# Two-layer hybrid backbone: modulation blocks moved between engines and stages

## The chip, the cores and the metric

One core of one Trainium2 chip runs the whole program in one launch. The metric is device time in microseconds. The kernel before takes 2973.64 us, the median of three runs (2973.43 to 2979.33).

## The reference

Two layers work on 256 latent tokens of width 2048. The first layer mixes with a gated linear recurrence beside a short convolution, the second with a Hyena long convolution; each is followed by a squared-ReLU feed-forward block of width 8192. All of it is fp32. What matters here:

```
sh1, sc1, g1, sh2, sc2, g2 = split(silu(c) @ ada_w[l] + ada_b[l], 6)     # per layer l
h = rmsnorm(x, norm_g[l, 0]) * (1 + sc1) + sh1
x = x + g1 * mixer(h)
x = x + g2 * square(relu((rmsnorm(x, norm_g[l, 1]) * (1 + sc2) + sh2) @ mlp_w1[l])) @ mlp_w2[l]
```

`ada_w` is 2 x 2048 x 12288 fp32 and is multiplied by one single vector per layer, so it is mostly a matter of streaming 192 MB. The Hyena filters come from a small network of position codes (`hyena_filters`: three layers of width 64 with sines, independent of the data).

## The kernel before, in words

**Stages.** The input projection and recurrence of layer 0; its output projection `ab_out`; feed-forward block `mlp(0)` (the first of the two); `hyena`, the third stage; then its output projection at the end of `hyena`; and `mlp(1)`, the second feed-forward block.

**Matrix products.** Weights arrive as 1 MB pieces `raw` (three buffers). ScalarE rounds each half to `whi`, VectorE forms the rest `wlo` (L151, L152), and TensorE makes three products of them with the split activations. In a feed-forward block `gemm_as` (L287) takes four such pieces for 512 outputs, and calls a hook after every piece. `mlp_body` goes through the hidden width in four quarters (`c`), with four passes of the first product and four of the second in each.

**Modulation blocks.** `ada_w` is cut into 192 blocks of 1 MB. Block number idx is l * 96 + ch * 16 + kt. A block whose number is not in `ON_PE` is a dot product on VectorE: one instruction of 2048 elements per partition with an accumulated output (L182). A block in `ON_PE` goes to TensorE instead: `ada_mm` makes 16 products of 32 output rows (L212), ScalarE copies the result out into `adas` (two buffers), and a later small product with `selr` sums the four row groups (L194), followed by an addition on VectorE (L195). These last two steps wait in a list, and `ada_flush` issues them at the next pump.

**Pumps.** All blocks from 32 on stand in one queue. `pump(n)` takes n of them, but never past `ada_stop`; `pump_rate(r)` adds r to a credit and pumps its whole part. The rates stand in `RATES`: ("m1", l) and ("m2", l) for the hooks of the feed-forward block of layer l, "hy" for the projections of the third stage. `pump_until` takes what a step needs. Before the change blocks 72 to 159 go to VectorE in `ab_out` (8) and in the first feed-forward block (80), 160 to 183 to TensorE in the third stage, and 184 to 191 to VectorE in the second feed-forward block. The loads go through SyncE's DMA queue, into `araw` (two buffers) in the feed-forward blocks and into `raw` elsewhere.

**Border of a feed-forward block.** `norm_apply` first makes the reciprocal root of the mean square (one small product, then twelve short VectorE instructions), then 16 tiles of three instructions on VectorE and ScalarE, which the first `gemm_as` waits for.

**Filter network.** `filter_net` runs two layers of the filter network on GpSimd alone, in compensated fp32 arithmetic, from the first stage on (L1050 to L1110, then a sine, L1159 to L1184). `filter_tail` is called in `mlp_body(0)` at c == 2, g == 0, before the second product of the third quarter: it transposes the result `fxn` on TensorE (L1127), multiplies (L1131), runs another sine on GpSimd in two halves and splits the outcome on VectorE (L1141, L1142).

**Order.** Each engine's instruction order is fixed at build time by a planner that goes by estimated times, dependences and the order of writing; on the chip each engine runs its own list strictly in order. `hold` ties a dot product behind the VectorE instruction written just before it.

Of the kernel before, what the change touches and what calls it, by code (L numbers as in the profile page):

```python
# [12 lines left out]
F32 = mybir.dt.float32  # L13
# [8 lines left out]
P = 128  # L22
D = 2048
# [4 lines left out]
LEVELS = (1, 2, 4, 8, 16, 32, 64)  # L28
KBLOCKS = (1, 2, 5, 8)
G = 2  # L30
RATES = {"gc": 0.35, "ab": 0.62, "y": 0, "gate": 0, "leash": 4, "tl": 1, "lo": 0.3, "hy": 0.5, "ho": 0.0, "ahead": 2,
         ("m1", 0): 0.65, ("m2", 0): 0.65, ("m1", 1): 0.15, ("m2", 1): 0.15}
SB = 8
ON_PE = set(range(32)) | set(range(56, 72)) | set(range(160, 184))

SM = {}
_o = 0
# [26 lines left out]
class Kernel:  # L64
# [111 lines left out]
    def ada_block(self, l, ch, kt):  # L176
# [3 lines left out]
        r = self.ada_load(l, ch, kt)  # L180
        if idx not in ON_PE:
            self.hold(nc.vector.scalar_tensor_tensor(out=r, in0=r, scalar=0.5, in1=self.sil, op0=ALU.mult,  # L182
# [236 lines left out]
    def norm_apply(self, l, i, slot):  # L419
        nc = self.nc  # L420
        bc = self.norm_rstd([self.ssum])
        self.new_h()
        a = l * 96 + i * 48
        for kt in range(KT):
            t = self.tmp(T, "cv0", 2)
            sh = self.mod[:, a + kt:a + kt + 1]
            nc.vector.scalar_tensor_tensor(out=t, in0=self.x[:, kt, :], scalar=self.gv[:, slot, kt:kt + 1], in1=bc,
                                           op0=ALU.mult, op1=ALU.mult)
            nc.scalar.activation(out=self.hhi(kt), in_=t, func=AF.Identity, bias=sh)  # L429
            nc.vector.scalar_tensor_tensor(out=self.hlo(kt), in0=t, scalar=sh, in1=self.hhi(kt).bitcast(F32),  # L430
                                           op0=ALU.add, op1=ALU.subtract)
# [4 lines left out]
    def build(self):  # L436
        nc, cp, I, tc = self.nc, self.cp, self.I, self.tc
        self.setup()
        with ExitStack() as st:
            self.pm = st.enter_context(tc.tile_pool(name="pm", bufs=1))  # L440
            with ExitStack() as sa:
                self.pa = sa.enter_context(tc.tile_pool(name="pa", bufs=1))
                self.layer0()
            with ExitStack() as sb:
                pb = sb.enter_context(tc.tile_pool(name="pb", bufs=1))
                self.make_sil(pb)
                self.ada_raw = lambda: pb.tile([P, D], F32, tag="araw", name="araw", bufs=2)
                self.pump_to(72)
                self.ada_stop = 160
                self.ab_out()  # L450
                self.mlp(0)
                self.ada_raw = None
        with ExitStack() as st:
            self.ph = st.enter_context(tc.tile_pool(name="ph", bufs=1))
            self.ada_stop = 184
            self.hyena()
        with ExitStack() as st:
            pb = st.enter_context(tc.tile_pool(name="pc", bufs=1))
            self.make_sil(pb)
            self.ada_raw = lambda: pb.tile([P, D], F32, tag="araw", name="araw", bufs=2)  # L460
            self.ada_stop = 192
            self.mlp(1)

    def layer0(self):
# [414 lines left out]
        for i in range(NH):  # L879
            acc = self.gemm(w1[16 + 3 * i], self.hhi, self.hlo, T)  # L880
            u = self.tmp(T, "cv0", 2)
            nc.scalar.activation(out=u, in_=acc[:, :T], func=AF.Copy)
            self.pump_rate(RATES["gc"])
            acc = self.gemm(w1[17 + 3 * i], self.hhi, self.hlo, T)
            nc.vector.tensor_tensor(out=u, in0=acc[:, :T], in1=u, op=ALU.mult)
            c = self.tmp(T, "cv1", 2)
            self.conv(u, c, self.s_("cw", i), self.s_("cw", 8 + i), self.s_("cw", 16 + i))
            self.pump_rate(RATES["gc"])
            acc = self.gemm(w1[18 + 3 * i], self.hhi, self.hlo, T)
            nc.vector.tensor_tensor(out=c, in0=acc[:, :T], in1=c, op=ALU.mult)  # L890
            self.hilo(c, self.uhi(8 + i), self.ulo(8 + i))
            self.pump_rate(RATES["gc"])
        self.drain()
# [5 lines left out]
    def ab_out(self):  # L899
        I = self.I  # L900
        for nt in range(KT):
# [3 lines left out]
            if nt < 13:  # L905
                self.pump_rate(RATES["ab"])
        self.dump("x0a", self.x)
# [73 lines left out]
    def mlp_body(self, l):  # L981
# [6 lines left out]
        for c in range(4):  # L988
            self.new_u()
            for g in range(4):  # L990
                rate = RATES["m1", l] if c or g else 0
                acc = self.gemm_as(I["m1"][l, c * 4 + g], self.hhi, self.hlo, lambda: self.pump_rate(rate))
# [6 lines left out]
            for g in range(4):  # L999
                if c == 3 and g == 2:  # L1000
                    self.pump_to(self.ada_stop)
                if c == 2 and g == 0 and l == 0:
                    self.filter_tail()
                rate = RATES["m2", l] if c < 3 or g < 3 else 0
                acc = self.gemm_as(I["m2"][l, c, g], self.uhi, self.ulo, lambda: self.pump_rate(rate))
# [465 lines left out]
def layout(a):  # L1471
# [6 lines left out]
    d["ada"] = c(a["ada_w"].reshape(2, D, 96, P).transpose(0, 2, 3, 1).reshape(192, P, D))  # L1478
    for i in ON_PE:
        blk = a["ada_w"][i // 96].reshape(KT, P, 96, P)[:, :, i % 96]  # L1480
# [55 lines left out]
```

## Time and profile before

The profiled execution took 2974.1 us; its span, from the first to the last instruction, is 2972.0 us.

| engine | busy us | share of the span |
|---|---|---|
| TensorE products | 2790.1 | 94% |
| TensorE weight loads | 2457.8 | 83% |
| VectorE | 2176.5 | 73% |
| ScalarE | 1246.6 | 42% |
| GpSimd | 1565.0 | 53% |

DMA moves 646 MB at a mean of 218 GB/s. The mean granted TensorE clock is 0.973 of full speed. Shares over the span mix stages with different limits, so the stage table in the rows below says more; a wait is always put down to the instruction that released it, and engine names in the rows are PE (TensorE), DVE (VectorE), ACT (ScalarE), POOL (GpSimd).

### The profile page before, as it was taken

Reading aid. Unit: us, or ns where it says so; the run is one execution under the profiler, and the core shown is the slowest. Engines: PE = TensorE matmul, PEld = TensorE weight load, DVE = VectorE, ACT = ScalarE, POOL = GpSimd, SP = SyncE. Lnnn points to the kernel's source line nnn. Section 1 sums busy time; section 2 is a strip of 40 time slices with the busy share of each in tenths; the row PEclk is TensorE's granted clock in tenths of the full one; section 3 lists DMA queues with packets and bytes.
Section 4 is the critical chain, followed back from the end, with each engine's and each line's share of the span. In section 5 each row is a group of like instructions: output and inputs, shape, how many; then the busy total and the mean of one; then the engine's idle time right before and its main releaser. Section 6 shows DMA issues by size and latency. Waiting matters only on the chain. (4 is left out here: it accounts for less than half of the span.)

```text
span 2972.0 us, 46189 instructions
## 1 busy us (share of the span) xinstructions
PE 2790.1 (94%) x18508; PEld 2457.8 (83%) x18508; DVE 2176.5 (73%) x2648; ACT 1246.6 (42%) x1660; POOL 1565.0 (53%) x1716
## 2 busy tenths in 40 slices
PE   5887999999989999998999899999989999999997
PEld 4777999889977888886888899998988888888885
DVE  4766659998798878876778899999765555545455
ACT  3221224343435444343444445545445444344443
POOL 5999999999999999997000445455100000000000
PEclk8998999999999999999999999999999999999998
DMA  5776545446757888875887445444545555555542
GB/s 206 279 264 237 189 145 191 160 153 235 259 216 269 320 304 302 312 297 224 315 308 267 169 159 182 168 182 166 196 170 199 218 217 187 187 182 189 186 180 110
DMA packets 97863, 646.48 MB, mean 218 GB/s; under 512 B 11673, under 2 KB 15833, under 8 KB 22257
## 3 DMA queue, kind: packets, MB, share of 16 engines
q1 hardware_dynamic: 96464, 640.35, 57.7%
q0 software_dynamic: 1184, 3.18, 0.7%
q8 instruction: 145, 2.38, 0.3%
q14 instruction: 70, 0.57, 0.1%
HBM read 641.39 MB, written 2.10 MB: 217 GB/s over the span
## 5 line engine op out<-in xcount | busy, mean ns | idle before, releaser
L152 DVE TENSOR_TENSOR wlo<-raw,whi 128x1024 fp32r<-128x1024 f32 (+1 forms) x778 | 1020.3, 1315 | 531.7 <-ACT whi L151 529.9
L151 ACT ACTIVATE whi<-raw 128x1024 fp32r<-128x1024 f32 (+1 forms) x806 | 843.5, 1049 | 1102.3 <-PE acc L287 713.3
L1030 POOL TENSOR_TENSOR xT<-xT,rstd 128x256 f32<-128x256 f32 x6 | 5.2, 900 | 853.3 <-DVE rstd L318 853.3
L287 PE MATMUL acc<-whi,hh 128*128 128x512 f32 x1024 | 403.2, 398 | 15.0 <-ACT hh L429 15.0
L266 PE MATMUL acc<-hh,whi 128*128 128x258 f32 (+1 forms) x1408 | 408.7, 290 | 0.0
L287 PE MATMUL acc<-whi,hl 128*128 128x512 f32 x1024 | 402.7, 398 | 3.1 <-DVE hl L430 3.1
L287 PE MATMUL acc<-whi,uh 128*128 128x512 f32 x1024 | 405.3, 396 | 0.0
L287 PE MATMUL acc<-whi,ul 128*128 128x512 f32 x1024 | 404.8, 395 | 0.0
L266 PE MATMUL acc<-hh,wlo 128*128 128x258 f32 (+1 forms) x1408 | 401.2, 285 | 3.4 <-DVE wlo L152 3.2
L266 PE MATMUL acc<-hl,whi 128*128 128x258 f32 (+1 forms) x1408 | 399.4, 284 | 0.0
L287 PE MATMUL acc<-wlo,uh 128*128 128x512 f32 x1024 | 282.0, 396 | 8.9 <-DVE wlo L152 8.9
L287 PE MATMUL acc<-wlo,hh 128*128 128x512 f32 x1024 | 280.1, 395 | 0.0
L266 PEld LDWEIGHTS acc<-hh,whi 128*128 128x128 f32 x1408 | 267.9, 190 | 7.4 <-issue 6.7
L266 PEld LDWEIGHTS acc<-hh,wlo 128*128 128x128 f32 x1408 | 267.5, 190 | 6.1 <-DVE wlo L152 4.2
L266 PEld LDWEIGHTS acc<-hl,whi 128*128 128x128 f32 x1408 | 269.0, 191 | 1.1 <-issue 0.9
L287 PEld LDWEIGHTS acc<-whi,hh 128*128 128x128 f32 x1024 | 193.4, 189 | 60.2 <-ACT hh L429 15.8
L182 DVE SCALAR_TENSOR_TENSOR araw<-araw,sil 128x2048 f32<-128x2048 f32 x96 | 237.9, 2479 | 0.2 <-DMA araw<-in_ada 0.2
L287 PEld LDWEIGHTS acc<-wlo,uh 128*128 128x128 f32 x1024 | 192.8, 189 | 54.1 <-DVE wlo L152 9.4
L287 PEld LDWEIGHTS acc<-whi,hl 128*128 128x128 f32 x1024 | 193.3, 189 | 47.4 <-DVE hl L430 4.7
L287 PEld LDWEIGHTS acc<-wlo,hh 128*128 128x128 f32 x1024 | 193.4, 189 | 45.4
L287 PEld LDWEIGHTS acc<-whi,uh 128*128 128x128 f32 x1024 | 193.0, 188 | 45.4 <-issue 0.3
L287 PEld LDWEIGHTS acc<-whi,ul 128*128 128x128 f32 x1024 | 193.0, 188 | 44.8
(358 smaller groups left out, 5803.3 us busy)
## 6 DMA issues: line engine op xcount, KB each, us to landing
raw<-in_m SPq DMA_DIRECT2D x256, 1024.0 KB, 4.8
araw<-in_ada SPq DMA_DIRECT2D x96, 1024.0 KB, 5.3
raw<-in_ada SPq DMA_DIRECT2D x93, 1024.0 KB, 4.9
raw<-in_w SPq DMA_DIRECT2D x71, 1024.0 KB, 4.9
raw<-in_hy SPq DMA_DIRECT2D x48, 1024.0 KB, 4.8
raw<-in_ho SPq DMA_DIRECT2D x16, 1024.0 KB, 4.8
raw<-in_w SPq DMA_DIRECT2D x12, 640.0 KB, 6.6
fr<-in_fw SPq DMA_DIRECT2D x16, 256.0 KB, 5.1
```

The costliest lines, as they stand in the source:

```text
L151: nc.scalar.activation(out=hi[:, :w], in_=src, func=AF.Copy)
L152: e.tensor_tensor(out=lo[:, :w], in0=src, in1=hi[:, :w].bitcast(F32), op=ALU.subtract)
L182: self.hold(nc.vector.scalar_tensor_tensor(out=r, in0=r, scalar=0.5, in1=self.sil, op0=ALU.mult, op1=ALU.mult, accum_out=self.mod[:, idx:i ...
L266: m = nc.tensor.matmul(acc[:, :n], lhsT=w[:, s], rhs=x(kt, n), start=hn == 0 and j == 0 and pn == 0, stop=hn == 1 and j == 7 and pn == 2).ins
L287: nc.tensor.matmul(acc[th], lhsT=x(kt)[:, th * P:(th + 1) * P], rhs=w[:, j * 512:(j + 1) * 512], start=kt == 0 and w is hi and x is xhi, s ...
L1030: e.tensor_tensor(out=self.x[:, nt, :], in0=self.x[:, nt, :], in1=rstd, op=ALU.mult)
```

## The change

Blocks 160 to 183 leave the third stage: the first feed-forward block now takes the queue up to 184. Of its 104 blocks the first six (80 to 85) go to TensorE, issued in one pump inside `norm_apply`, right after the small product and the reciprocal root; the other 98 are dot products, at a rate of 0.84 instead of 0.65 per hook. The third stage pumps nothing. The last eight blocks (184 to 191) go to TensorE in the second feed-forward block: six in `norm_apply`, two by rate. That block no longer builds the vector `sil`, which only dot products use, and has four `araw` buffers instead of two. The host lays a block of `ada_w` out by whether it is in `ON_PE`.

```diff
-RATES = {"gc": 0.35, "ab": 0.62, "y": 0, "gate": 0, "leash": 4, "tl": 1, "lo": 0.3, "hy": 0.5, "ho": 0.0, "ahead": 2,
-         ("m1", 0): 0.65, ("m2", 0): 0.65, ("m1", 1): 0.15, ("m2", 1): 0.15}
+RATES = {"gc": 0.35, "ab": 0.62, "y": 0, "gate": 0, "leash": 4, "tl": 1, "lo": 0.3, "hy": 0.0, "ho": 0.0, "ahead": 2,
+         ("m1", 0): 0.84, ("m2", 0): 0.84, ("m1", 1): 0.15, ("m2", 1): 0.15}
 SB = 8
-ON_PE = set(range(32)) | set(range(56, 72)) | set(range(160, 184))
+ON_PE = set(range(32)) | set(range(56, 72)) | set(range(80, 86)) | set(range(184, 192))
...
     def norm_apply(self, l, i, slot):
         nc = self.nc
         bc = self.norm_rstd([self.ssum])
+        self.pump(6)
         self.new_h()
...
                 self.pump_to(72)
-                self.ada_stop = 160
+                self.ada_stop = 184
                 self.ab_out()
                 self.mlp(0)
...
             pb = st.enter_context(tc.tile_pool(name="pc", bufs=1))
-            self.make_sil(pb)
-            self.ada_raw = lambda: pb.tile([P, D], F32, tag="araw", name="araw", bufs=2)
+            self.ada_raw = lambda: pb.tile([P, D], F32, tag="araw", name="araw", bufs=4)
             self.ada_stop = 192
             self.mlp(1)
```

## Rows read from the trace of the kernel before

**Rows 1.** Windows by stage: busy PE, PEld, DVE, ACT, POOL, then PEclk, DMA, GB/s.
```profile
905.00:1344.00 439.00, 439.00 (x1940) 356.29 (x1938) 361.47 (x293) 201.93 (x232) 431.83 (x374) 1.00 0.81 306
...
1405.00:1640.00 235.00, 233.15 (x1069) 191.26 (x1069) 185.99 (x219) 107.55 (x135) 5.19 (x3) 0.99 0.76 289
1640.00:2130.00 490.00, 455.66 (x4194) 440.42 (x4192) 443.54 (x641) 243.50 (x395) 224.55 (x153) 0.98 0.46 171
...
2207.00:2224.00 17.00, 7.96 (x27) 6.03 (x26) 14.14 (x32) 5.95 (x11) 0.00 (x0) 0.70 0.17 62
2224.00:2948.00 724.00, 724.00 (x3205) 588.28 (x3204) 375.44 (x364) 331.58 (x388) 0.00 (x0) 1.00 0.52 189
```

**Rows 2.** Dot products (line 182), 866:1344 and 1344:1405 us: min/median/max ns, starts.
```profile
L182 DVE SCALAR_TENSOR_TENSOR araw<-araw,sil x51: 2372/2548/2831, 905.2 to 1341.9; 128x2048 f32<-128x2048 f32 x51
L182 DVE SCALAR_TENSOR_TENSOR araw<-araw,sil x5: 2372/2551/2553, 1341.9 to 1383.4; 128x2048 f32<-128x2048 f32 x5
```

**Rows 3.** Waits of TensorE, 870 to 1600 us: total, times, longest.
```profile
PE acc L287 <- DVE wlo L152: 8.9, 1, 8.9
PE acc L287 <- ACT hh L429: 8.7, 1, 8.7
PE aux L1127 <- POOL fxn L1184: 4.7, 1, 4.7
```

**Rows 4.** Timeline of GpSimd: start, duration, line, tiles.
```profile
932.36 2.51 POOL L1055 TENSOR_TENSOR fwl<-fw,fwh 128x128 f32<-128x128 f32 x1
...
938.64 2.51 POOL L1101 TENSOR_TENSOR ft<-fp,ft 128x128 f32<-128x128 f32 x1
...
1313.90 0.46 POOL L1101 TENSOR_TENSOR ft<-fp,ft 128x128 f32<-128x128 f32 x1
...
1325.79 2.14 POOL L1164 TENSOR_TENSOR sfp<-sfp,sfe 128x128 f32<-128x128 f32 x1
...
1392.54 0.46 POOL L1164 TENSOR_TENSOR sfp<-sfp,sfe 128x128 f32<-128x128 f32 x1
```

**Rows 5.** Timeline of VectorE at the same times.
```profile
932.00 2.55 DVE L182 SCALAR_TENSOR_TENSOR araw<-araw,sil 128x2048 f32<-128x2048 f32 x1
...
938.28 2.55 DVE L182 SCALAR_TENSOR_TENSOR araw<-araw,sil 128x2048 f32<-128x2048 f32 x1
```

**Rows 6.** Timelines at the filter tail: GpSimd, VectorE and TensorE.
```profile
1348.74 0.42 PE L1127 MATMUL aux<-ident,fxn 128*64 128x128 f32 x1 [4.70 <-POOL fxn L1184]
...
1358.45 0.30 POOL L1159 TENSOR_SCALAR sfp<-cv 128x128 f32<-128x128 f32 x1 [9.77 <-DVE cv L1133]
...
1403.71 0.29 DVE L1141 CAST h3h<-cv 128x256 fp32r<-128x256 f32 x1 [14.36 <-POOL cv L1184]
...
1406.85 2.07 PE L287 MATMUL acc<-wlo,uh 128*128 128x512 f32 x4 [8.92 <-DVE wlo L152]
```

**Rows 7.** Third stage: windows of L212, of tile adas; L195; in the chain, shares.
```profile
1640.00:2130.00 490.00, 28.05 (x768) 20.67 (x768) 0.98 0.46 171
1640.00:2130.00 490.00, 6.68 (x48) 7.39 (x48) 6.50 (x24) 0.98 0.46 171
L195 DVE TENSOR_TENSOR mod<-aux,sm x40: 141/146/159, 451.5 to 2115.2; 128x1 f32<-128x1 f32 x40
2104.78 1.01 PE aux L212 x32
by line: DVE p L931 13.4%; DVE wlo L152 12.7%; DVE yl L158 8.3%; issue 7.2%; DVE y L1332 6.6%; POOL H L1270 4.5%; DVE tf L1247 4.1%; DVE p L933 4.0%; DVE cv L1298 3.6%; DVE y L1330 3.5%; DVE Z L1270 3.3%; ACT whi L151 2.7%; ACT p L928 2.6%;
by line: PE acc L266 33.7%; PE aux L1344 6.4%; DVE wlo L152 6.4%; DVE yl L158 6.2%; PE aux L1209 5.9%; DVE p L931 5.0%; DVE y L1332 4.2%; issue 3.4%; DVE cv L1298 3.4%; DVE y L1330 3.3%; DVE Z L1270 2.5%; PE aux L212 2.0%; POOL tf L1259 2.0
```

**Rows 8.** Timeline of TensorE at the border of the second feed-forward block.
```profile
2217.40 1.22 PE L287 MATMUL acc<-whi,hh 128*128 128x512 f32 x2 [6.37 <-ACT hh L429]
...
2222.50 0.63 PE L287 MATMUL acc<-whi,hh 128*128 128x512 f32 x2
...
2225.28 0.63 PE L287 MATMUL acc<-whi,hh 128*128 128x512 f32 x2
```

## The prediction, made before the change was timed

> **What bounds the kernel now.** I read the stage table first, then the waits of TensorE, then the timelines around the longest waits. The table [rows 1] is to be read by stage, since every stage has another limit. In the first feed-forward block up to 1344 us TensorE is busy all the time (439.0 of 439.0 us), VectorE 361.5 us, and GpSimd 431.8 us: GpSimd, too, has nothing left. The reader is to see that two engines are full here, and that VectorE's 18% of idle time is shared by both of them. From 1405 us to the end of that block GpSimd is idle and TensorE full. In the third stage (1640 to 2130 us) neither TensorE (455.7 of 490) nor VectorE (443.5) is full. The second block (2224 to 2948) is TensorE's alone.
>
> The waits of TensorE in the first block [rows 3] are three: 8.7 us at its border for the first normalized rows, 4.7 us for `fxn`, and 8.9 us behind VectorE. The last two are one matter. GpSimd works since the first stage on the small network that makes the Hyena filters (`filter_net`); `filter_tail`, which stands at the start of the third quarter's second product, needs its result. TensorE comes to that place at 1344.0 and GpSimd ends at 1348.7 [rows 6]. So the end of this stretch is set by GpSimd already, by a margin of 4.7 us; TensorE's full row before it hides that.
>
> **What a dot product costs GpSimd.** This is the term on which my forecast rests. A modulation dot product on VectorE lasts 2.55 us while GpSimd works [rows 2, 5]. The GpSimd instruction that meets it lasts 2.51 us, where the same line takes 0.46 us with VectorE idle [rows 4, 5]: 2.05 us lost; for the shorter dot product at 1325 it is 2.14 against 0.46, 1.68 us lost [rows 4]. I take 1.9 us per dot product.
>
> The Trainium skill has a rule on this (SBUF — State Buffer, "Who interferes with whom"): a VectorE instruction with two SBUF inputs and a GpSimd one that reads SBUF exclude each other, and the second fully blocks. Taken by the letter, a dot product costs GpSimd all of its 2.55 us, the term below would be 36.7 instead of 27.4 us, and the whole 3001 us. The rows say less, because one GpSimd instruction's own work is let through with each.
>
> **The change part by part.**
>
> *More dot products before the tail.* `filter_tail` comes after 20 matrix passes of 4 pumps each, the first four without a rate: 76 pumps. At 0.65 they bring 49 dot products (the trace has 51 between 905 and 1344 us [rows 2], two having slipped ahead); at 0.84 they bring 64. That is 14.4 more (76 x 0.19), each 2.55 us on VectorE, together 37 us, which raises it to about 398 of 439 us: it still fits beside TensorE, so no stall by VectorE is priced. For GpSimd it is 14.4 x 1.9 = 27.4 us. The filter network ends so much later, and TensorE waits for it: while TensorE stands, VectorE soon does too, and GpSimd then works at its free pace, which is what the 1.9 us are counted in. **+27.4 us**; bounds 13 x 1.68 = 22 and 15 x 2.05 = 31.
>
> *The second half of the tail.* The sine that follows (1358 to 1404 us) meets 4 dot products now (of the five in rows 2 the first began before it); VectorE's next instruction waits 14.4 us for it, TensorE 8.9 us behind that [rows 3, 6]. At 0.84 it meets 1.2 more: 1.2 x 1.9 = **+2.3 us** (0 to 4).
>
> *The clock.* After a wait of some 9 us at a border the first 12 products take 5.10 us instead of 2.78 [rows 8]: the granted clock was 0.70 there [rows 1], the lower level in part. A wait of 32 us at the tail, in place of 4.7, should cost about as much: **+2 us** (0 to 3).
>
> *The border of the first block.* Six blocks go into the 8.7 us in which TensorE waits [rows 3], at 1.01 us each [rows 7]; two are loaded by then, four more follow through two buffers. I cost this at nothing, gain or loss: what is won or lost here up to 1344 us is covered by the wait for GpSimd, which counts from its own start. Without that cover it is worth -2 us of clock, or up to +6 us if the last two loads are waited for in TensorE's order. DMA goes from a share of 0.81 [rows 1] to some 0.90 (15 MB more on 134) in this block and is under the same cover.
>
> *The third stage loses its 24 blocks.* They hold TensorE for 28.05 us, and their small second products for 6.68 us [rows 7]. Were all of that on the path, 34.7 us would go; were the path VectorE's alone, nothing. The chain runs over VectorE in the stretch up to 1960 us (no L212 among its largest shares) and over TensorE in the last third [rows 7]. I take the engine that is fuller afterwards, VectorE at about 440 us (it loses only 24 additions of 0.15 us [rows 7]), and let it keep the idle time that the fuller one has now (490 - 455.7 = 34 us): 474 us, **-16 us** (0 to -34.7).
>
> *The border of the second block.* Six blocks, 6.1 us, into the 9.0 us that TensorE idles there [rows 1] save the clock's 2.3 us [rows 8]; the two that remain (2.0 us) and eight second products (6.68 / 24 = 0.28 us each [rows 7], 2.2 us) come into a block in which TensorE is full: **+1.9 us**, from -3 to +6 if a late load holds the queue. `make_sil` and eight dot products fall away from VectorE, which has 349 us to spare there [rows 1]: nothing. Four early loads instead of two lie beside the output projection: nothing.
>
> Sum: 27.4 + 2.3 + 2 - 16 + 1.9 = **+17.6 us** on the profiled execution's 2974.1, so 2991.7; the median of the runs is 0.5 us below that execution: **2991 us**.
>
> **Rivals.**
>
> *The filter network isn't late (faster).* If dot products cost GpSimd nothing more, because it makes its time up in VectorE's idle 77 us, the tail keeps its waits and the rest remains: 2974.1 - 16 + 1.9, about **2960 us**. It decides from the point where a dot product costs GpSimd less than 14.1 / 14.4 = 1.0 us. For it: GpSimd gets through during every idle piece of VectorE. Against it: GpSimd has no idle time before 1344 us to give (431.8 of 439), and every one of the dot products in rows 5 met a stretched GpSimd instruction.
>
> *The third stage gives back all of TensorE's time (no change).* With -34.7 instead of -16 the sum is -1.1: about **2973 us**. For it: TensorE is the fuller engine there, and its chain leads the last third. Against it: VectorE's sum alone is 440 us, and the stage would have to end 15 us above it, with filter work that passes in turns between engines.
>
> *The blocks at the borders hold the queue.* Six blocks are issued without a flush between them, with two `adas` and four PSUM buffers: the third can't be copied out until the first one's second product ran. If at the second border this and the loads delay the first products, +6 instead of +1.9: **2995 us**, slower like my forecast.
>
> **How the numbers follow.** What a measurement here can tell from no change is about 0.2%, 6 us. The forecast, the late filter network with a third stage that gives about half: 0.55, alone 2980 to 3003. The held queue with it: 0.12. The third stage giving all: 0.16. The network not late: 0.17. The range leaves out most of the last case and the ends of the others: 2971 to 3004. Slower by over 0.2% is the first two, 0.66 (a little of their lower edge falls within); within 0.2% 0.17; faster 0.17.
>
> **What would show it.** Right: TensorE waits some 30 us for `fxn` at the tail, GpSimd's last `fxn` near 1376 us, and that stretch with VectorE idle; GpSimd instructions of the same count before it; a third stage about 474 us long. Wrong: a tail reached with a wait below 10 us kills the first term; a third stage under 460 us the third; a second border longer than its 17 us means held queues. The whole is wrong if the instruction order puts the tail's transposes elsewhere, which I can't see from the profile of before.

## The result, and the profile after

The changed kernel takes 3013.05 us (median of four runs, 3007.40 to 3016.42); the kernel before took 2975.85 us beside it. The ratio is 1.0121 (95% interval 1.0109 to 1.0134): 37 us slower, where the forecast was 17 us slower. The profiled execution's span grew from 2972.0 to 3011.2 us. Five marks divide it; each but the last is the start of one instruction:

| mark | before | after | change of the stretch |
|---|---|---|---|
| transposes of `fxn` on TensorE (L1127) | 1348.7 | 1376.6 | +27.9 |
| `h3h` on VectorE (L1141) | 1403.7 | 1434.4 | +2.8 |
| table split at the start of the third stage (L1195) | 1638.8 | 1669.4 | -0.1 |
| product of the second border's sum (L324) | 2210.3 | 2239.9 | -1.0 |
| end | 2972.0 | 3011.2 | +9.6 |

The stage table of the kernel after, with the columns of [rows 1]; the third stage and what follows lie some 30 us later:

```profile
905.00:1344.00 439.00, 439.00 (x1939) 356.48 (x1939) 399.41 (x322) 201.94 (x232) 434.09 (x320) 1.00 0.90 340
1344.00:1405.00 61.00, 33.03 (x135) 26.16 (x134) 26.75 (x27) 12.22 (x14) 46.48 (x72) 0.75 0.42 155
1405.00:1640.00 235.00, 224.71 (x988) 182.10 (x987) 180.59 (x203) 100.93 (x120) 29.15 (x44) 0.98 0.81 302
1670.00:2160.00 490.00, 429.45 (x3383) 420.42 (x3382) 451.04 (x616) 237.22 (x371) 220.39 (x153) 0.96 0.34 122
2237.00:2254.00 17.00, 10.91 (x178) 9.10 (x177) 9.90 (x27) 4.11 (x10) 0.00 (x0) 0.77 0.75 294
```

Up to 1344 us nothing seems amiss: TensorE is full as before. What has changed is GpSimd's count, 320 instructions instead of 374 [rows 1] in nearly the same busy time (434.1 and 431.8 us). The bill comes in the next row, where TensorE works 33 of 61 us. In the third stage TensorE is busy 26 us less than in [rows 1], and VectorE 7.5 us more, though it has fewer instructions.

The dot products in the first block (866 to 1344 us), answering to [rows 2]; then TensorE's waits (870 to 1600 us: total, times, longest), answering to [rows 3]:

```profile
L182 DVE SCALAR_TENSOR_TENSOR araw<-araw,sil x65: 2279/2549/2835, 907.8 to 1343.6; 128x2048 f32<-128x2048 f32 x65
```

```profile
PE aux L1127 <- POOL fxn L1184: 28.0, 1, 28.0
PE acc L287 <- DVE wlo L152: 10.3, 1, 10.3
PE aux L194 <- ACT adas L191: 4.0, 2, 2.9
PE aux L212 <- DMA araw<-in_ada: 2.5, 1, 2.5
```

The timelines at the filter tail, answering to [rows 6]: GpSimd's last step of `fxn`, TensorE, VectorE, TensorE.

```profile
1376.13 0.45 POOL L1184 TENSOR_TENSOR fxn<-sfq,sfp 128x128 f32<-128x128 f32 x1
1376.64 0.42 PE L1127 MATMUL aux<-ident,fxn 128*64 128x128 f32 x1 [27.97 <-POOL fxn L1184]
...
1434.43 0.29 DVE L1141 CAST h3h<-cv 128x256 fp32r<-128x256 f32 x1 [14.86 <-POOL cv L1184]
...
1437.44 2.08 PE L287 MATMUL acc<-wlo,uh 128*128 128x512 f32 x4 [10.29 <-DVE wlo L152]
```

In square brackets stands the idle time before the instruction and who ended it: 28.0 us for `fxn` instead of 4.7. While TensorE stands, VectorE is idle as well and GpSimd has the time to itself (the five engines' columns as in [rows 1]):

```profile
1348.70:1376.60 27.90, 0.00 (x0) 0.00 (x0) 0.49 (x1) 0.00 (x0) 25.46 (x54) 0.56 0.17 61
```

The second border, TensorE first, then ScalarE, VectorE and SyncE's queue, answering to [rows 8]:

```profile
2239.90 1.19 PE L324 MATMUL aux<-ssum,onesd 128*128 128x256 f32 x2 [2.76 <-DVE ssum L417]
2241.02 4.55 PE L212 MATMUL aux<-araw,silt 128*32 128x128 f32 x128
2245.50 0.61 PE L194 MATMUL aux<-selr,adas 128*128 128x2 f32 x4
2249.43 1.80 PE L212 MATMUL aux<-araw,silt 128*32 128x128 f32 x32 [3.33 <-DMA araw<-in_ada]
2251.16 1.02 PE L194 MATMUL aux<-selr,adas 128*128 128x2 f32 x4
2252.04 1.20 PE L287 MATMUL acc<-whi,hh 128*128 128x512 f32 x2
```

```profile
2247.19 0.91 ACT L430 ACTIVATE hh<-cv,mod 128x256 fp32r<-128x256 f32 x2 [0.77 <-DVE cv L428]
2251.79 0.28 ACT L191 ACTIVATE adas<-aux 128x128 f32<-128x128 f32 x1 [3.69 <-PE aux L194]
2253.23 0.51 ACT L430 ACTIVATE hh<-cv,mod 128x256 fp32r<-128x256 f32 x1 [1.16 <-DVE cv L428]
```

```profile
2251.79 0.16 DVE L195 TENSOR_TENSOR mod<-aux,sm 128x1 f32<-128x1 f32 x1 [4.24 <-PE aux L194]
```

```profile
2243.02 2.95 SPq L163 DMA_DIRECT2D araw<-in_ada  x4
```

Four blocks pass at once; the fifth one's matrix was asked for only at 2243 us, when the first `araw` buffer came free. The first two tiles of `hh` are there at 2248.1 us, but TensorE's list has the fifth block ahead of the first product, which so begins 12.1 us behind the sum's product instead of 7.1. ScalarE, too, is held: its copy into `adas` waits for the second products, and the next tile of `hh` stands behind it. So is VectorE, whose addition (L195) waits 4.2 us for a second product with the next tiles behind it; the second products (L194) stand behind the fifth block in TensorE's list.

### The profile page after: what moved, and what is told of

The parts are those of the page before. It is cut to its first block, busy times and chain, and to the rows that moved or that the text cites. A ratio compares the mean times of both kernels' runs of the same rounds, so it can differ in the third digit from the quotient of the medians.

```text
span 3011.2 us, 45490 instructions
## 1 busy us (share of the span) xinstructions
PE 2792.5 (93%) x18168; PEld 2461.2 (82%) x18168; DVE 2214.3 (74%) x2659; ACT 1242.9 (41%) x1649; POOL 1588.7 (53%) x1716
## 4 chain that ended last, share of the span: by engine, by line
POOL 45%; PE 39%; DVE 11%; issue 2%; DMA 1%; ACT 1%; SPq 0%; DVEq 0%; ACTq 0%; POOLq 0%
PE acc L287 31%; POOL fe L1091 6%; PE acc L266 5%; POOL fq L1090 5%; POOL ft L1098 3%; POOL ft L1102 3%; POOL facc L1104 3%; POOL ft L1103 3%; POOL ft L1099 3%; POOL ft L1100 3%; POOL ft L1101 3%; POOL ft L1097 2%; DVE wlo L152 2%; POOL fp L1086 2%; POOL fwh L1050 2%
## 5 line engine op out<-in xcount | busy, mean ns | idle before, releaser
L287 PE MATMUL acc<-whi,hh 128*128 128x512 f32 x1024 | 405.6, 399 | 0.2 <-ACT hh L430 0.2
L287 PE MATMUL acc<-whi,uh 128*128 128x512 f32 x1024 | 405.5, 396 | 0.0
L287 PE MATMUL acc<-whi,ul 128*128 128x512 f32 x1024 | 405.5, 396 | 0.0
L287 PE MATMUL acc<-whi,hl 128*128 128x512 f32 x1024 | 404.7, 398 | 0.0
L287 PE MATMUL acc<-wlo,uh 128*128 128x512 f32 x1024 | 283.3, 397 | 10.3 <-DVE wlo L152 10.3
L287 PE MATMUL acc<-wlo,hh 128*128 128x512 f32 x1024 | 279.4, 395 | 0.0
L182 DVE SCALAR_TENSOR_TENSOR araw<-araw,sil 128x2048 f32<-128x2048 f32 x106 | 266.8, 2517 | 0.0
L287 PEld LDWEIGHTS acc<-wlo,uh 128*128 128x128 f32 x1024 | 193.3, 189 | 55.7 <-DVE wlo L152 10.7
L287 PEld LDWEIGHTS acc<-whi,hh 128*128 128x128 f32 x1024 | 193.9, 190 | 45.2 <-ACT hh L430 0.8
L287 PEld LDWEIGHTS acc<-whi,uh 128*128 128x128 f32 x1024 | 193.3, 189 | 45.2 <-issue 0.2
L287 PEld LDWEIGHTS acc<-whi,ul 128*128 128x128 f32 x1024 | 193.2, 189 | 45.2 <-issue 0.3
L287 PEld LDWEIGHTS acc<-wlo,hh 128*128 128x128 f32 x1024 | 192.7, 188 | 45.2
L287 PEld LDWEIGHTS acc<-whi,hl 128*128 128x128 f32 x1024 | 193.4, 189 | 43.2 <-issue 0.4
```

Source lines behind the costliest of these rows:

```text
L287: nc.tensor.matmul(acc[th], lhsT=x(kt)[:, th * P:(th + 1) * P], rhs=w[:, j * 512:(j + 1) * 512], start=kt == 0 and w is hi and x is xhi, s ...
```

## The experiments

A gain or loss of a whole run is told by its ratio to the kernel before on the same chip; stretches are taken between the marks above. "Third stage" is from L1195 to the second border's L324. Line numbers are those of the kernel before; an edit can shift them by a few. One execution of each kernel is profiled, and the runs of one kernel lie 2 to 16 us apart, so a few us in a stretch of a single trace prove little by themselves.

**The rate alone** (e1_rate84).

```diff
-         ("m1", 0): 0.65, ("m2", 0): 0.65, ...
+         ("m1", 0): 0.84, ("m2", 0): 0.84, ...
```

> The kernel before with one number changed: rate 0.84 instead of 0.65 in the first feed-forward block (the same 80 dot products there, only earlier; the same blocks in the third stage). Theory (dot products before the filter tail delay GpSimd by 1.9 us each): 64 instead of 49 come before the tail, TensorE's wait for fxn grows from 4.7 to about 32 us, fxn ends near 1376 us, and the whole takes 27 to 31 us more, about 3004 us; nothing is given back behind the tail. Rival (the wait of the changed kernel comes from the blocks at the border or from 104 MB instead of 80): the wait stays near 5 us and the time within 6 us of before.

Measured: 3009.01 us, ratio 1.0105 (1.0088 to 1.0122). The row of TensorE's wait:

```profile
PE aux L1127 <- POOL fxn L1184: 39.4, 1, 39.4
```

`fxn` ends at 1380.1 us, 31.4 later than before, and the third stage begins 33.8 later; third stage and second border are nearly as before (572.6 us, and 761.8 to the end; before 571.6 and 761.7). So this one number in `RATES` makes most of the loss. The wait is 11.4 us longer than in the changed kernel: `fxn` ends 3.5 us later, and TensorE comes to it at 1340.7 instead of 1348.7 us. Of these 8.0 us it brings 2.9 along from ahead of the block (the border's L324 at 863.1 and 866.0); the other 5.1 are the six blocks that the first border lacks here, which were under the cover that the prediction gave them.

The higher rate also brings more loads before the tail (a DMA share of 0.90 instead of 0.81), which could be a rival to the dot products. The GpSimd instructions tell the two apart. Between the first and the second `fxn` the chain has 965 of them in both kernels; over the shortest time that an instruction of their kind takes in these traces, those that meet a dot product lose 211 us instead of 169, and all others 274 instead of 289. What is longer is the first group alone.

**The old rate up to the tail, a higher one behind it** (e2_rate65, from the changed kernel).

```diff
                     self.filter_tail()
+                    RATES["m1", 0] = RATES["m2", 0] = 1.2
```

(with 0.65 up to there)

> The changed kernel, but at rate 0.65 up to the filter tail and 1.2 behind it, so that all 98 dot products still run in the first feed-forward block. Theory: the wait for fxn falls from 28 us to between 4 and 8 us, the stretch behind the tail has room on VectorE (186 of 235 us busy before) and loses at most 5 us, so the whole is 20 to 28 us faster than the changed kernel, 2985 to 2993 us, still slower than before by the 10 us of the second border. Rival (VectorE is too full with 98 dot products, wherever they stand): the wait goes, but TensorE loses 15 us or more behind the tail.

Measured: 3001.87 us, 1.0082 (1.0066 to 1.0099). The wait for `fxn` is gone (`fxn` ends at 1341.9, and TensorE reaches the transposes at 1349.3), but the time is a miss: the third stage takes 582.9 us instead of 570.5. The stretch behind the tail is 1.6 us longer than before (236.7 instead of 235.0 from `h3h` to L1195), so the rival's loss of 15 us there didn't come either. The dot products pushed behind the tail don't end in time. The last of them stand on VectorE inside the third stage's first reciprocal root (window behind the tail, then VectorE's timeline):

```profile
1409.00:1646.00 237.00, 231.59 (x1042) 189.14 (x1043) 203.88 (x238) 105.92 (x133) 2.37 (x1) 0.98 0.89 332
```

```profile
1652.72 4.45 DVE L182 SCALAR_TENSOR_TENSOR araw<-araw,sil 128x2048 f32<-128x2048 f32 x1
...
1665.26 0.29 DVE L313 TENSOR_SCALAR rstd<-rs_q 128x256 int32<-128x256 int32 x1
1665.58 0.42 DVE L316 TENSOR_TENSOR rs_q<-rstd 128x256 f32<-128x256 f32 x1
1665.93 2.29 DVE L182 SCALAR_TENSOR_TENSOR araw<-araw,sil 128x2048 f32<-128x2048 f32 x1
```

The DMA engines were at 0.89 there, and the filters' first loads were issued at 1668 instead of 1620 us, behind the blocks' loads.

**The third stage without its blocks** (e3_noblocks, from the kernel before; 24 modulation values are constants instead).

```diff
         idx = l * 96 + ch * 16 + kt
+        if 160 <= idx < 184:
+            return
```

> The kernel before without blocks 160 to 183 at all: they are neither loaded nor computed (their modulation values are constants), everything else stays. This is the third stage's part of the change alone. Theory now (VectorE and the steps tied to it set the third stage): from the splitting of the transform table to the small product at the second border 571.5 us become 568 to 572, the whole within 4 us of before. What the prediction had: 16 us less, about 2959 us. Rival (TensorE's time is all on the path): 30 us less.

Measured: 2973.73 us, 0.9985 (0.9975 to 0.9994); the third stage takes 571.3 us, before it 571.6. In the window 1640:2130 TensorE is busy 430.9 us instead of 455.7 [rows 1]: 24.7 us of its work are worth 0.3. That drop is also less than the 34.7 us that the prediction summed from the blocks' own rows.

The other traces agree, with more spread: the third stage takes 571.6 to 574.0 us in the four kernels that have these blocks (before, e1, e8, e10), and 568.6 to 571.3 in the seven without (after, e3, e6, e7, e9, e11, e12; e2 is left out for its late dot products). The blocks are worth some 2.6 us by the means, far from 16.

**The third stage with less on VectorE** (e4_noconv, from the kernel before; the right-hand term of its convolutions, 48 instructions and 31.2 us of VectorE, is left out).

```diff
-            self.conv(t, dst, self.s_("hs", nt), self.s_("hs", 48 + nt), self.s_("hs", 96 + nt))
+            self.conv(t, dst, self.s_("hs", nt), self.s_("hs", 48 + nt), self.s_("hs", 96 + nt), right=False)
```

> The kernel before with the third stage's right-hand convolution term left out (48 VectorE instructions of line 933, 31 us of VectorE; nothing else). Theory (VectorE sets the third stage): 571.5 us of third stage become 545 to 557. Rival (TensorE sets it, with its 24 blocks): 566 to 572. If both bind in turn: about 560.

Measured: 2960.65 us (one run); third stage 555.7 us, 15.9 less: half of what VectorE was spared.

**Both left out** (e5_noboth).

> The kernel before without blocks 160 to 183 (their 24 values are set to 0.01) and without the right-hand term of the convolution in the third stage (48 VectorE instructions): the first left out alone gave a third stage of 571.3 us, the second alone 555.7, neither 571.5. Theory (VectorE and the steps tied to it set the third stage, also when they are shorter by 31 us): 552 to 556 us, 2956 to 2961 in all. Rival (TensorE is the next bound right behind it, so the blocks' 24 us come through once VectorE is relieved): 538 to 546 us, 2942 to 2950 in all.

Measured: 2953.02 us (one run); third stage 549.8 us, between the two expectations. Its windows 1640:2130, without the blocks, without the term, without both:

```profile
1640.00:2130.00 490.00, 430.94 (x3376) 421.51 (x3375) 447.16 (x615) 238.60 (x373) 225.65 (x153) 0.95 0.35 122
```

```profile
1640.00:2130.00 490.00, 467.86 (x4322) 453.02 (x4322) 429.23 (x609) 251.55 (x407) 219.61 (x153) 0.99 0.50 181
```

```profile
1640.00:2130.00 490.00, 447.16 (x3557) 439.37 (x3556) 438.29 (x586) 247.72 (x384) 222.13 (x153) 0.96 0.38 130
```

Without the blocks TensorE is simply idle more; without the term it is busier, 467.9 us, because the same work passes in less time. The blocks lay in waits: they are worth 0.3 us with VectorE as it is, 5.9 us (555.7 - 549.8) once VectorE is relieved.

**The second border alone** (e10_border, from the kernel before).

```diff
-ON_PE = ... | set(range(160, 184))
+ON_PE = ... | set(range(160, 184)) | set(range(184, 192))
...
         bc = self.norm_rstd([self.ssum])
+        if l == 1:
+            self.pump(6)
...
-            self.make_sil(pb)
-            self.ada_raw = lambda: ... bufs=2)
+            self.ada_raw = lambda: ... bufs=4)
```

> The kernel before, with the second border of the changed kernel alone: blocks 184 to 191 on TensorE, six of them right behind the normalizer's sum, four buffers for their loads, no new table sil. Theory (TensorE works in order, comes to the fifth block before its matrix has landed, and the two small buffers of ScalarE's copies hold ScalarE's queue ahead of hh): from the sum's product (L324) to the first product of the block 12 us instead of 7.1, another 4 us up to the first L972, the rest as before: 8 to 10 us in all, some 2986 us if the kernel before takes 2977. Rival (the 10 us come from how the third stage ends in the changed kernel, not from the border): 7 to 8 us from sum to first product, 2975 to 2979 us.

Measured: 2983.88 us, 1.0020 (1.0010 to 1.0030). From the sum's product to the first product 9.5 us instead of 7.1, and 766.0 to the end instead of 761.7: +4.3, short of the 8 to 10 of the theory, though not the rival's nothing. The same row as in the changed kernel is there, with half its wait:

```profile
2225.88 1.08 PE L212 MATMUL aux<-araw,silt 128*32 128x128 f32 x32 [1.64 <-DMA araw<-in_ada]
```

By accident this run shows more of the first block. TensorE entered it 11.5 us earlier than in the kernel before (L324 at 854.7 instead of 866.2), and all of that became waiting, since GpSimd came no earlier (`fxn` ends at 1352.9 instead of 1348.7):

```profile
PE aux L1128 <- POOL fxn L1185: 20.7, 1, 20.7
```

**Four blocks instead of six at the second border, and six buffers instead of four** (e6_border4 and e7_six_loads, both from the changed kernel).

```diff
-        self.pump(6)
+        self.pump(6 if l == 0 else 4)
```

> The changed kernel with four blocks at the second border instead of six (the other four go in at the rate of the block, 0.15). Theory of the missing matrix: the four are loaded long before, so TensorE waits for no load, and the first product comes 7 to 8.5 us behind the sum instead of 12.1; the products up to L972 lose 2 to 4 us less; four blocks later on cost 1 us each at most: 4 to 8 us off, 3005 to 3009 us. Rival (each block at the border costs its 1.1 us and its steps on VectorE, load or no load): a third of the loss goes, 3 us off, 3010.

```diff
-name="araw", bufs=4)
+name="araw", bufs=6)
```

> The changed kernel with six buffers for the matrices instead of four, so all six blocks at the second border are loaded before it; all else is the same. Theory of the missing matrix: the wait of 3.3 us for it goes, the copies behind it leave ScalarE's queue earlier, first product 8 to 9 us behind the sum instead of 12.1, 3 to 5 us off, 3008 to 3010 us. Rival (the pairs of small copies alone hold ScalarE's queue): first product still 11 to 12 us behind the sum, no change, 3013 us.

Measured: 3010.17 us, 1.0108 (1.0090 to 1.0125), and 3011.38 us, 1.0112 (1.0092 to 1.0131); as whole times neither can be told from the changed kernel. The border can: in both, no load is waited for, and the first product comes 8.0 and 8.8 us behind the sum's product instead of 12.1; to the end it takes 766.4 and 764.7 us instead of 771.3. Both profiled executions reached the third stage some 5 us later than the changed kernel's, with `fxn` at fault (waits of 30.3 and 31.5 us), which hides the gain. TensorE with six buffers:

```profile
2245.07 5.37 PE L212 MATMUL aux<-araw,silt 128*32 128x128 f32 x128
2250.37 0.61 PE L194 MATMUL aux<-selr,adas 128*128 128x2 f32 x4
2251.44 1.95 PE L212 MATMUL aux<-araw,silt 128*32 128x128 f32 x64 [0.46 <-DVE mod L195]
2253.32 0.50 PE L287 MATMUL acc<-whi,hh 128*128 128x512 f32 x1
```

Its first twelve products take 2.9 us (from 2253.3 to 2256.2) at a granted clock of 1.00, where the kernel before needs 5.1 [rows 8] at 0.52: TensorE stood 0.5 us ahead of them instead of 6.4.

**The filter's tail written later** (e9_after_split, from the changed kernel).

```diff
-                if c == 2 and g == 0 and l == 0:
+                if c == 2 and g == 2 and l == 0:
                     self.filter_tail()
```

(and h3h, h3l in a function of their own, called at c == 3, g == 2 of the first product)

> The changed kernel with filter_tail taken apart and put later: its transposes, its product and its sine ahead of the third group of that quarter's second product instead of the first, its last two steps (h3h, h3l) ahead of the third group of the last quarter. All dot products stay where they are. Theory (the 28 us that TensorE waits for fxn, and the 9 to 10 behind the table's end, are waits of the order alone): both go, 35 to 38 us off, some 2976 us, and not over 2985. Rival (the first stage is bound by its loads and by VectorE at a rate of 0.84, so what TensorE doesn't wait for there it waits for the split weights later): 10 to 20 us off, 2993 to 3003 us.

Measured: 3003.90 us, 1.0082 (1.0063 to 1.0101). By its number the rival has it (by the ratios 12 us off, 10 to 20 expected), but not by its reason: 192 products were meant to pass, but the planner put the transposes only 101 later (2048 instead of 1947 products of L287 stand between the border's sum and them), presumably where its estimate had `fxn` ready, and TensorE waited 22.4 us there instead of 28.0. The wait behind the table's end stayed too, 9.4 us. The expectation had taken the place in the text for the place on the engine.

**The same, tied by hand** (e11_after_late, from the changed kernel).

```diff
+        behind = self.latest(nc.tensor.engine)
         for a in range(2):
-            nc.tensor.transpose(out=tp[:64, ...], in_=h2[:, a, :], ...)
+            i = nc.tensor.transpose(out=tp[:64, ...], in_=h2[:, a, :], ...)
+            self.hold(i.ins, behind)
```

(called at c == 3, g == 0 of the first product; h3h and h3l tied likewise on VectorE at c == 3, g == 1 of the second; by the traces the transposes stand 357 products later than in the changed kernel, and 101 later in the run before, where the text below has 296 and 78)

> The changed kernel with filter_tail taken apart and tied by hand, transposes 296 products later on TensorE (some 71 us) and h3h, h3l into the last quarter's second product. All dot products and blocks stay. Run e9_after_split moved the transposes by 78 products only, because the planner set them where it thought fxn ready, and kept waits of 22.4 and 9.4 us; here neither wait can stay. Theory: the third stage starts (table split, L1195) at 1632 to 1640 us instead of 1669, and the whole takes 2976 to 2986 us, the border's 10 us being what is left over the kernel before. Rival (at a rate of 0.84 the loads, 0.90 of the DMA engines, and VectorE, 399 of 439 us, set the first block): L1195 at 1650 or later, 2992 to 3002 us.

Measured: 2970.24 us, 0.9980 (0.9970 to 0.9990): 42 us less than the changed kernel by the ratios (1.0121 - 0.9980), and faster than the kernel before. The third stage begins at 1624.5 us, earlier than either theory had it; the trace is of the fastest of the twelve runs, 5.8 us under their median. TensorE's row (its waits for `fxn` and `wlo` are gone):

```profile
1344.00:1640.00 296.00, 296.00 (x1405) 244.37 (x1404) 250.48 (x280) 134.43 (x165) 146.92 (x125) 1.00 0.82 301
```

**The same in the kernel before** (e8_split), rates and blocks untouched. The edit is that of the run before, at other places: `filter_tail` is called at c == 2, g == 2 of the second product, and `h3h` and `h3l` at c == 3, g == 3 of the first. In the trace the transposes stand 165 products later than in the kernel before, where the text below has 122.

> The kernel before (rates, blocks and borders untouched), with filter_tail taken apart: its transposes tied behind the products written before them, 122 products later on TensorE, and its last two steps (h3h, h3l) tied on VectorE into the last quarter. Theory (TensorE's waits of 4.7 for fxn and 8.9 for wlo behind the table's end are waits of the order alone, and nothing else is late there): both go, and 1 to 2 us of slow clock with them, 13 to 16 us off: a ratio of 0.995. Rival (VectorE or the loads of the first feed-forward block set the time there, and TensorE waits for split weights instead): half comes back, 5 to 8 us off, a ratio of 0.998.

Measured: 2957.68 us, 0.9934 (0.9917 to 0.9952), the fastest kernel of this study, 19.7 us under the kernel before and over 50 under the changed one. It won 18.6 us ahead of the third stage (1620.2 instead of 1638.8): 13.6 are the two waits, and 2.3 lie ahead of the block (L324 at 864.0 instead of 866.2). For the 2.7 that remain, the slower clock behind the waits is the likely part, but not shown alone. The window 1344:1405, before and here:

```profile
1344.00:1405.00 61.00, 49.23 (x208) 39.23 (x207) 32.21 (x34) 18.18 (x18) 46.39 (x63) 0.96 0.58 221
```

```profile
1344.00:1405.00 61.00, 61.00 (x263) 48.79 (x263) 45.83 (x44) 23.43 (x23) 27.73 (x34) 1.00 0.79 297
```

**The tail tied late, and the second border of the kernel before** (e12_late_border1).

> As e11_after_late (the changed kernel with the filter's tail tied late), but with the second border of the kernel before: no blocks there, blocks 184 to 191 as dot products at a rate of 0.15 in the last block, table sil made again, two buffers. Theory (the second border costs the changed kernel 5 to 10 us: the sum's product to the end took 771.3 and in e11 769.6 us, in the kernel before 761.7): 761 to 763 us from the sum's product to the end, 2960 to 2965 us in all, a ratio of 0.9955. Rival (the eight dot products and sil that come back cost as much, since it was only a matter of which engine works): 767 to 770 us, 2970 us, no gain over e11.

Measured: 2964.91 us, 0.9962 (0.9950 to 0.9974). From the sum's product to the end 762.0 us, as the theory had it, 7.6 less than with the blocks (769.6). What is left of the change here is its first block, third stage and first border: 1625.3 us to the third stage where the run before this one has 1620.2, and a third stage of 568.8 us instead of 572.4. With the wait for GpSimd gone, this kernel comes to the third stage 5.1 us later, of which 1.9 lie ahead of the block (L324 at 865.9 and 864.0) and 3.2 in it (six blocks at its border, 18 dot products more, a DMA share of 0.92, and a tail at another place); the empty third stage gives 3.6. The trace is of the fastest of seven runs here; by the ratios of all runs this kernel lies some 8 us behind the run before (0.9962 against 0.9934). Either way there was nothing to win.

## Why the prediction was wrong

By terms, forecast and measured between the marks:

| step | forecast | measured |
|---|---|---|
| more dot products before the tail | +27.4 | +27.9 |
| second half of the tail, and the clock | +4.3 | +2.8 |
| rest of the first block | 0 | -0.1 |
| third stage without its blocks | -16 | -1.0 |
| second border and block | +1.9 | +9.6 |
| sum | +17.6 | +39.2 |

*The mechanism of the first term was right.* GpSimd's filter network is what TensorE waits for, and dot products delay it: 14 more of them [rows 2] cost 27.9 us, 2.0 each, where 1.9 was taken from [rows 4, 5]. That the sum fits to half a microsecond is luck: at the old rate `fxn` ends between 1341.9 and 1352.9 us in six traces, at the new one between 1376.6 and 1381.8 in four. Counted from the end of the first layer's `fxn`, the chain takes 971.2 us instead of 941.4, 2.1 per dot product. The rate alone shows it, and tying the tail late takes it away. That *the filter network isn't late* is refuted. Taken by the letter, the Trainium skill's rule that the second of two such instructions is fully blocked (SBUF — State Buffer, "Who interferes with whom") would make the 14 cost 14 x 2.55 = 35.7 us, an estimate; the trace shows 27.9, and the measurement decides. The rows agree with the blocking itself: the GpSimd instruction of 932.36 begins 0.36 us behind the dot product's start and ends 0.32 us behind its end [rows 4, 5]. What the estimate leaves out is that one GpSimd instruction comes through with each dot product.

*The border of the first block* was rightly put at nothing: TensorE reached the tail 4.7 us later (1348.7 against 1344.0), and its wait of 28.0 us is that much shorter than the 32 expected there. The price without that cover was put at up to +6; counted from the border's sum (L324), TensorE reaches the tail after 482.7 us instead of 477.8, so it is 4.9.

*The third stage's term failed, and makes 15 of the missing 22 us.* "I take the engine that is fuller afterwards ... and let it keep the idle time that the fuller one has now" assumes that TensorE's fuller row set the stage. It didn't: its blocks fell into waits, most of them for VectorE, and taking them out left the waits longer. Behind L1358's output TensorE waits 17.4 us in the changed kernel's third stage (1670 to 2240 us), 7.4 before (1640 to 2210). The lower bound, "were the path VectorE's alone, nothing", was in the text; the chain's shares [rows 7] had VectorE's lines ahead up to 1960 us. That TensorE led the last third was read as a price for its blocks. The runs without them and without VectorE's term show that it wasn't: 0.3 against 15.9 us.

*The second border's term makes the other 7.7 us.* The rival *the blocks at the borders hold the queue* named the mechanism, and gave it 0.12 and +6. I summed 6.1 us of blocks into 9.0 us of idle time, as if the order let the first product pass, and booked 2.3 us of clock as won. In the trace the first product comes 5.1 us later. The twelve products from there, with the sixth block among them, take 6.2 us instead of 5.1, at a granted clock of 0.65, so no clock was won. All that follows is 3.4 us longer; for the two later blocks and all the second products 4.2 were forecast.

Two things hold the first product: the fifth block's load, which can't start until a buffer is free, and the short steps of the blocks (`adas` copies, second products, additions) ahead of `hh` and its like in the engines' lists. With six buffers 3.0 us of loss are left: the first product is 1.8 us late, the twelve products win 2.2 us of clock (2.3 were forecast), and the rest is 3.5 us longer. With no blocks 0.3 is left (762.0 against 761.7).

With four buffers and six blocks the loss is 4.3 to 9.6 us in five kernels, in two groups. Where TensorE stood 0.7 and 1.6 us for the load (e9, e10), the twelve products and the sixth block took 4.2 us at a granted clock of 1.00, and the loss is 5.1 and 4.3. Where it stood 2.7 to 3.3 us (e2, e11 and the changed kernel), they took 6.2 to 7.1 us at 0.55 to 0.65, and the loss is 7.1 to 9.6. What sets the length of that wait was not settled.

## What to carry to other kernels

A full row of a stage table doesn't make an engine the bound: take its work out once, and if the stage keeps its length, what you moved away was free where it was. Before work is moved onto an engine, ask whose instructions it stretches (here GpSimd's, from 0.46 to 2.51 us) and which late consumer waits for that neighbour; here a wait of 4.7 us was the sign of a network with no slack, and taking that consumer's place in the order was worth more than any choice of rates tried here. Place in the program text isn't place on the engine where a planner orders: tie it, then look.

## What the runs showed of the hardware

GpSimd slows down far more when TensorE doesn't stop. With the tail tied late in the changed kernel, `fxn` ends at 1424.1 us, 47 us later than in the changed kernel itself, and 77 dot products instead of 65 run beside its chain: the 28 us in which TensorE stood had let VectorE fall idle (0.5 of 27.9 us busy), and GpSimd had gone at its free pace (0.45 us an instruction instead of up to 2.5). A wait for GpSimd is in part its own remedy, so its length understates how late GpSimd is.

TensorE's granted clock follows its gaps: a mean of 0.75 of full speed, between its two levels of 1.2 and 2.4 GHz, in the window around the 28 us wait, and 1.00 there once the wait was gone. Four `wlo` products took 2.08 us behind the wait of 10.3 us, and 1.09 us in the next group of four, 4.4 us further on. At the second border the products ran at 1.00 behind waits of 0.7 and 1.6 us, and at 0.55 to 0.65 behind waits of 2.7 to 3.3 us.
